# Gate products from GpSimd to VectorE and to an earlier place, the attention's division on ScalarE, and weight sums of the branch projection made in DRAM

## The chip, the cores and the metric

One core of a Trainium2 chip runs the kernel. The metric is the device time of one execution in microseconds (us). The core has five engines with a queue of instructions each: TensorE (PE in the profile, its weight loads PEld), VectorE (DVE), ScalarE (ACT), GpSimd (POOL) and SyncE (SP). Each works its own queue in order and waits for the others by semaphores. SP, ACT and POOL can also issue DMA transfers; a transfer that adds into its destination is issued by POOL here.

## The reference, cut to what matters

```python
shift, scale, gate = jnp.split(silu_c @ w_ada[l] + b_ada[l], 3, axis=-1)
h = _modulate(_rmsnorm(xs, norm_g[l]), shift[:, None], scale[:, None])
p = h @ w_l                       # q, k, v, z_a, u_b, z_b, g_a, g_b: 9216 columns
attn = _attention(q, concat(k, kc), concat(v, vc))     # 12 heads, 4 key heads
y_a = (attn * silu(z_a)) @ w_pa
y_b = (_fourier_mix(u_b) * silu(z_b)) @ w_pb
y = (sigmoid(g_a) * y_a + sigmoid(g_b) * y_b) @ w_o
out = _rmsnorm(xs + gate[:, None] * y, final_g)
```

There are 512 latent tokens, 256 context tokens and 2048 channels; all is float32. `gate` is a vector of 2048 numbers, a product of a row of 2048 with a 2048x2048 matrix. It is used only at the very end, on the output of the last product. This vector is called the modulation gate below, to keep it apart from the branch gates `g_a`, `g_b`.

## The kernel before, in words

**Stages, in order of time.** (1) The start computes shift, scale, the token norms, `h`, and the Fourier branch. (2) Eight groups, g0 to g7 (the table `KINDS`): three of q and z_a, two of g_a, one of keys and values (g5, number `KV`, which also makes the context's), two of g_b. (3) The attention, 48 steps (12 heads, 4 blocks of 128 queries), a loop of 51 turns. (4) Two branch products of `attn * silu(z_a)` with `w_pa` (groups 10 and 11). (5) Two output products with `w_out` (groups 8 and 9) and the final norm.

**A group** multiplies 512x2048 activations by a 2048x1024 slab of weights with seven products instead of eight (a Strassen scheme with the names P1, Q5, P2, Q6, P7, Q3, Q4). Each product has four pieces of weights, 128x1024 numbers or 512 KB each; in the branch products it is three pieces. A float32 matmul is made of three passes over rounded parts: ScalarE makes the high part of a piece (`split_from`, L166, tile `whi`), VectorE the low part (L167, `wlo`), and `mm3` (L318 to L320) issues the three. A piece thus gives 12 matmuls of 512 columns.

**Weights are streamed.** `todo` lists the pieces in order of use. `start_load` (L203) takes the next one, asks SP for its load into a free slot of `raw_pools` (tile `wr`) and puts it on `ahead`; it does so whenever a slot is free. There are four such slots in the pool `wp`, and two more, `raw0` and `raw1`, from the end of the start on; `raw1` is lent out for other things from g4 on, and two slots of the pool `gvp` are added in g6 and g7. Some products use sums of weight blocks: the buffers `R` (`chain`) hold a block to which POOL's DMA adds the next (L273). The fifth product, P7, of the branch groups takes a sum of two blocks: SP loads one into a slot, then POOL issues a DMA that adds the other into the same slot (L206, the argument `onto`).

**The attention loop.** Step i has `scores(i)`: PE multiplies 128 queries with 768 keys, VectorE finds the row's maximum (L1233), ScalarE takes the exponential and the row's sum (L1235). `turn(i-1)` transposes the probabilities on PE (L1251) and splits them (L166, L167, `pth`, `ptl`). `values` multiplies with the values every second step. `divide(i-1)` takes the reciprocal of the sum (L1244) and multiplies it into the 128x128 block of silu(z_a), both on VectorE (L1245). Beside it run the fillers: the 64 parts of `y_b`, for which POOL's queue loads the gates (L1178) and stores the results (L1202), and the loads of the next head's q and z (L1085).

**The modulation gate before.** It is also made in the attention loop, by `gate_unit`. The transposed gate weights come as 32 pieces of 128x1024 (`w_gate`), two for each of 16 blocks. For each block POOL multiplies both pieces with the row silu(c) (L1329, twice), adds them (L1332), and ScalarE sums the result along the row (L1333, `accum_out`). Four such units are issued in three steps from step 2 on, so that the last is issued at step 37. Each piece is asked for with `ask_gate`, out of the order of `todo`, when the piece before it of the same half is taken up.

**Order.** The program is written out by Python loops; the framework's scheduler places the instructions of each engine in an order of its own from the dependencies and its estimates. Branch results are brought back by `branch_done` (a DMA that adds `y_b` from DRAM, L1350) and five ticks later by `turn_merged` (PE transposes, L1359); `job` counts one tick for each piece of weights.

## Time and profile before

| what | us |
|---|---|
| time, median of 3 runs | 1392.07 |
| lowest and highest of the 3 | 1389.04, 1392.32 |
| time of the profiled execution | 1390.56 |
| its span, first to last instruction | 1388.8 |
| PE busy in it | 1302.5 (94%) |
| DVE busy | 1014.4 (73%) |
| ACT busy | 689.6 (50%) |
| POOL busy | 292.2 (21%) |

The busy time of an engine is the time in which it executes, not that in which it waits; matmuls overlap, so that PE shows as busy whenever one is in flight. `PEclk` is the share of full speed that the clock of TensorE was granted. Issuing a DMA isn't counted as busy on SP and ACT. All times of the trace are counted from the start of the span.

### The profile page before, as it was taken

What the parts mean: (1) busy time and instruction counts of PE and PEld (TensorE: products, weight loads), DVE (VectorE), ACT (ScalarE), POOL (GpSimd) and SP (SyncE); (2) the same over time, 40 slices, a digit from 0 to 9 for tenths busy, and PEclk for the clock granted to TensorE, in tenths of its full rate; (3) what the DMA queues carried; (4) which work ended last, traced back from release to release, by engine and by line L of the source; (5) the groups of instructions that cost most, each with busy time, mean ns of one, the idle gap of its engine ahead of it and who ended that gap; (6) DMA issues with size and microseconds to landing.
All of it is one profiled execution on the core that took longest, in us unless ns stands there. A gap on an engine that the chain in (4) does not pass through costs nothing.

```text
span 1388.8 us, 17575 instructions
## 1 busy us (share of the span) xinstructions
PE 1302.5 (94%) x6522; PEld 1062.5 (77%) x6522; DVE 1014.4 (73%) x1277; ACT 689.6 (50%) x1063; POOL 292.2 (21%) x280
## 2 busy tenths in 40 slices
PE   7999999999999999999999986788699997999997
PEld 3676888888888888888888865677688776778885
DVE  4666899878787867474867658687788665778676
ACT  5222565555555545443545544455456544555544
POOL 0110010212110010010201157654630212121310
PEclk9999999999999999999999999899999998999999
DMA  9897687897888899776698775453563898899986
GB/s 386 334 377 287 210 190 249 206 254 201 252 241 247 294 255 284 178 184 200 168 313 229 224 258 165 143 177 108 180 156 100 229 250 178 248 211 222 215 215 176
DMA packets 101990, 312.25 MB, mean 225 GB/s; under 512 B 9616, under 2 KB 32912, under 8 KB 97552
## 3 DMA queue, kind: packets, MB, share of 16 engines
q0 software_dynamic: 28560, 117.46, 36.0%
q1 hardware_dynamic: 48720, 163.65, 34.0%
q10 hardware_dynamic: 24624, 30.02, 6.2%
q8 instruction: 51, 0.84, 0.2%
q14 instruction: 35, 0.29, 0.1%
HBM read 280.15 MB, written 30.94 MB: 224 GB/s over the span
## 4 chain that ended last, share of the span: by engine, by line
PE 75%; DMA 8%; POOL 6%; DVE 5%; issue 3%; ACT 2%; POOLq 0%; SPq 0%; DVEq 0%; ACTq 0%
PE x L319 8%; PE x L320 8%; PE x L318 8%; PE y L319 7%; PE y L320 7%; PE y L318 7%; PE banks L318 6%; PE banks L320 6%; PE banks L319 6%; POOL wr L1329 3%; DMA wr<-in_w_gate 3%; DMA s<-yb_d 3%; POOL wr L1332 2%; PE pd L510 2%; DMA wr<-in_w_pab 2%
## 5 line engine op out<-in xcount | busy, mean ns | idle before, releaser
L167 DVE TENSOR_TENSOR wlo<-R,whi 128x1024 fp32r<-128x1024 f32 x138 | 167.9, 1221 | 90.2 <-ACT whi L166 89.6
L166 ACT ACTIVATE whi<-R 128x1024 fp32r<-128x1024 f32 x138 | 145.9, 1059 | 170.4 <-PE banks L320 46.8
L167 DVE TENSOR_TENSOR wlo<-wr,whi 128x1024 fp32r<-128x1024 f32 (+1 forms) x123 | 150.7, 1229 | 60.9 <-ACT whi L166 60.9
L166 ACT ACTIVATE whi<-wr 128x1024 fp32r<-128x1024 f32 (+1 forms) x123 | 128.4, 1049 | 101.3 <-PE y L320 36.7
L318 PE MATMUL banks<-whi,s 128*128 128x512 f32 x396 | 158.9, 401 | 9.9 <-DVE ev L833 4.9
L319 PE MATMUL banks<-wlo,s 128*128 128x512 f32 x396 | 156.9, 396 | 0.9 <-DVE wlo L167 0.9
L320 PE MATMUL banks<-whi,s 128*128 128x512 f32 x396 | 156.9, 396 | 0.0
L273 POOL DMA_DIRECT2D R<-in_w_g x64 | 55.3, 863 | 419.9 <-DVE wlo L167 234.6
L318 PE MATMUL x<-whi,s 128*128 128x512 f32 x352 | 137.2, 390 | 0.0
L320 PE MATMUL x<-whi,s 128*128 128x512 f32 x352 | 137.0, 389 | 0.0
L319 PE MATMUL x<-wlo,s 128*128 128x512 f32 x352 | 136.9, 389 | 0.0
L318 PE MATMUL y<-whi,s 128*128 128x512 f32 x316 | 123.0, 389 | 0.0
L319 PE MATMUL y<-wlo,s 128*128 128x512 f32 x316 | 122.9, 389 | 0.0
L320 PE MATMUL y<-whi,s 128*128 128x512 f32 x316 | 122.8, 389 | 0.0
L318 PEld LDWEIGHTS banks<-whi,s 128*128 128x128 f32 x396 | 75.6, 191 | 26.3 <-issue 5.3
L166 ACT ACTIVATE s<-wr 128x512 fp32r<-128x512 f32 (+2 forms) x93 | 61.7, 678 | 67.4 <-PE y L319 16.3
L319 PEld LDWEIGHTS banks<-wlo,s 128*128 128x128 f32 x396 | 75.6, 191 | 15.6 <-DVE wlo L167 1.3
L320 PEld LDWEIGHTS banks<-whi,s 128*128 128x128 f32 x396 | 75.4, 190 | 15.6
L167 DVE TENSOR_TENSOR s<-wr,s 128x512 fp32r<-128x512 f32 (+2 forms) x93 | 69.2, 771 | 24.7 <-ACT s L166 24.5
L320 PEld LDWEIGHTS x<-whi,s 128*128 128x128 f32 x352 | 66.1, 188 | 13.8
L319 PEld LDWEIGHTS x<-wlo,s 128*128 128x128 f32 x352 | 66.1, 188 | 13.6
L318 PEld LDWEIGHTS x<-whi,s 128*128 128x128 f32 x352 | 66.1, 188 | 13.6
(289 smaller groups left out, 2986.7 us busy)
## 6 DMA issues: line engine op xcount, KB each, us to landing
wr<-in_w_g SPq DMA_DIRECT2D x128, 512.0 KB, 4.9
R<-in_w_g POOLq DMA_DIRECT2D x64, 512.0 KB, 6.6
wa<-in_w_ss POOLq DMA_DIRECT2D x26, 1024.0 KB, 8.2
R<-in_w_g SPq DMA_DIRECT2D x32, 512.0 KB, 4.9
wr<-in_w_gate SPq DMA_DIRECT2D x32, 512.0 KB, 4.2
wr<-in_w_pab SPq DMA_DIRECT2D x26, 512.0 KB, 5.4
wr<-in_w_o SPq DMA_DIRECT2D x24, 512.0 KB, 7.3
R<-in_w_o POOLq DMA_DIRECT2D x24, 512.0 KB, 7.9
```

The lines of the kernel that those rows point to most:

```text
L166: first = nc.scalar.activation(hi, src, ACT.Copy)
L167: return first, nc.vector.tensor_tensor(lo, src, hi.bitcast(F32), op=ALU.subtract)
L273: nc.gpsimd.dma_start(chain[e.pc], e.nxt, accum_op=ALU.add)
L318: nc.tensor.matmul(o, ah, bh, start=start, stop=False, skip_group_check=cont)
L319: nc.tensor.matmul(o, ah, bl, start=False, stop=False, skip_group_check=cont)
L320: nc.tensor.matmul(o, al, bh, start=False, stop=stop, skip_group_check=cont)
L510: last = nc.tensor.matmul(acc[32 * j : 32 * j + 32, :256], c2[:, 8 * h + k, :], w[:, k, :], start=n < 4, stop=n >= KK - 4)
L1329: nc.gpsimd.tensor_tensor(w, w, crow[part], op=ALU.mult)
L1332: nc.gpsimd.tensor_tensor(w, w, gw[1], op=ALU.add)
```

## The change

It has four parts.

1. **The gate's products move to VectorE.** Each of the 32 pieces is now handled by one instruction, `scalar_tensor_tensor`, which multiplies it by 0.5 and by the row, and sums along the row into a column of `gparts` (`use_gate`, in the new file L1091). POOL's two multiplications and its addition, and ScalarE's summation, are gone; one small addition of the two halves of `gparts` is new.
2. **28 of the 32 move into the groups.** A new table `GATE_AT` names the piece of the product after which a gate piece is used: three each in g1 and g2, one each in g3 and g4, six in g5, six in g6, eight in g7. The piece stands in `todo` behind the weights it follows and takes a slot of `raw_pools` like them. The row's halves are loaded and put through silu in g0 and g1, and in g6. The first half lies in `raw0`, which is no slot for weights from P7 of g0 until the sixteenth gate piece is done in g6; the second half lies in `raw1`. The last four gate pieces stay in the attention, at steps 2 to 22.
3. **The division** in the attention loop, a multiplication of a 128x128 block with a column, goes from VectorE to ScalarE. The reciprocal stays.
4. **The sums for P7 of the branch groups are made early.** In steps 3 to 20 of the attention, `weight_sum` makes six sums of two blocks: POOL loads one block into a free buffer (L1379), adds the other by DMA (L1380), and stores the sum to DRAM (`p7_d`, L1381). P7's pieces then are plain loads of SP from there. `turn_merged` comes six ticks after its result, no longer five.

```diff
+GATE_AT = ([(g, n, 1) for g in (1, 2) for n in ("P2", "Q6", "Q3")] + [(3, "Q5", 1), (4, "P2", 1)]
+           + [(5, n, 1) for n in ("P1", "P2", "Q6", "P7", "Q3", "Q4")] + [(6, n, 1) for n in ONE_GROUP if n != "Q5"]
+           + [(7, n, 1) for n in ONE_GROUP] + [(7, "Q6", 3)])
+    p7_d = dsc.tile([2, 3, P, 1024], F32, name="p7_d")
...
-            if e.onto is not None:
-                nc.gpsimd.dma_start(raw, e.onto, accum_op=ALU.add)
...
-                stream(key, [part(1)], 1024, 2, pc=pc, onto=part(2))
+                stream(key, [p7_d[g - BRANCH_A, pc]], 1024, 2, pc=pc)
...
+                q = None if self.last else GATE_AT.get((self.g, name, pc))
+                if q is not None:
+                    use_gate(q, get(("gate", q)))
+                    if q == KK - 1:
+                        raw_pools.append((rp, 1, "raw0", 1))
...
-    def use_gate(q):
-        w = get_aside(("gate", q))
+    def use_gate(q, w):
         with tc.issue_after(last_split[-1][1].ins):
             nc.vector.scalar_tensor_tensor(w, w, 0.5, crow[q // KK], op0=ALU.mult, op1=ALU.mult,
                                            accum_out=gparts[:, q : q + 1])
...
-        nc.vector.tensor_scalar(z, z, r, None, op0=ALU.mult)
+        nc.scalar.mul(z, z, r)
...
-            nc.gpsimd.tensor_tensor(w, w, crow[part], op=ALU.mult)
-            nc.gpsimd.tensor_tensor(w, w, gw[1], op=ALU.add)
-            nc.scalar.activation(w, w, ACT.Copy, scale=0.5, accum_out=gparts[:, kb : kb + 1])
...
-        after(5, lambda: turn_merged(j, half))
+        after(6, lambda: turn_merged(j, half))
...
+    def weight_sum(n):
+        i, pc = divmod(n, 3)
+        t, w = take((1024,)), BranchWeights(i)
+        part = lambda i: w[CHAIN[i][0], CHAIN[i][1], pc]
+        nc.gpsimd.dma_start(t, part(1))
+        summed.append((t, lambda: nc.gpsimd.dma_start(t, part(2), accum_op=ALU.add),
+                       lambda: nc.gpsimd.dma_start(p7_d[i, pc], t)))
...
+        if 3 <= i < 21:
+            n, step = divmod(i - 3, 3)
+            if step == 0:
+                weight_sum(n)
+            else:
+                summed[-1][step]()
+            if step == 2:
+                give(summed.pop()[0])
+        if 2 <= i < 26 and i % 6 in (2, 4):
+            n, last = NGATE + (i - 2) // 6, i % 6 == 4
+            if not last:
+                ask_gate(n)
+            else:
+                use_gate(n, get_aside(("gate", n)))
```

What it moves is seen in the queues. First POOL, early in the attention, before: `wr` are gate pieces, `crow` and `s_6426` the two halves of the row, `qz_d` is q and z of a head, `g_d` the gates of the filler.

```order
L1329 TENSOR_TENSOR wr_7009<-wr_7009,s_6426 128x1024
L1329 TENSOR_TENSOR wr_7011<-wr_7011,crow_6424 128x1024
L1332 TENSOR_TENSOR wr_7011<-wr_7011,wr_7009 128x1024
L1329 TENSOR_TENSOR wr_7139<-wr_7139,s_6426 128x1024
L1085 DMA s_7014<-qz_d 128x1024
L1329 TENSOR_TENSOR wr_7141<-wr_7141,crow_6424 128x1024
L1332 TENSOR_TENSOR wr_7141<-wr_7141,wr_7139 128x1024
L1329 TENSOR_TENSOR wr_7228<-wr_7228,s_6426 128x1024
L1202 DMA yb_d<-R_1303 128x1024
L1329 TENSOR_TENSOR wr_7230<-wr_7230,crow_6424 128x1024
```

POOL at the start of the attention in the new kernel: `p_d` is the DRAM buffer of the sums, L1379 the load, L1380 the load that adds, L1381 the store, L1099 the load of a head.

```order
L1379 DMA s_6641<-in_w_pab 128x1024
L1200 DMA R_1304<-g_d 128x1024
L1200 DMA R_1305<-g_d 128x1024
L1099 DMA s_6588<-qz_d 128x1024
L1380 DMA s_6641<-in_w_pab 128x1024
L1099 DMA s_6727<-qz_d 128x1024
L1379 DMA s_6773<-in_w_pab 128x1024
L1381 DMA p_d<-s_6641 128x1024
L1380 DMA s_6773<-in_w_pab 128x1024
L1379 DMA s_6883<-in_w_pab 128x1024
L1381 DMA p_d<-s_6773 128x1024
L1099 DMA s_6885<-qz_d 128x1024
```

No arithmetic on 128x1024 is left on POOL there; in its place stand transfers that depend on one another, and the load of a head (`s_6885`) behind them.

Next DVE in g7, at the splits of the chained sums of Q6 and the first of P7, before: L167 is the low part of a split (a piece is split whole into `wlo`, or in two halves into `s`).

```order
L167 TENSOR_TENSOR s_233<-R_1302,s_232 128x2x256
L167 TENSOR_TENSOR s_346<-R_1302,s_345 128x2x256
L167 TENSOR_TENSOR s_494<-R_1303,s_493 128x2x256
L167 TENSOR_TENSOR s_610<-R_1303,s_609 128x2x256
L167 TENSOR_TENSOR wlo_6071<-R_1304,whi_6070 128x1024
L167 TENSOR_TENSOR wlo_6092<-R_1305,whi_6091 128x1024
L167 TENSOR_TENSOR wlo_6111<-wr_6032,whi_6110 128x1024
```

The same place in the new kernel: L174 is the split, L262 the difference of a piece of P7 and its chained sum (L258 before), L1091 the gate.

```order
L174 TENSOR_TENSOR s_234<-R_1303,s_233 128x2x256
L262 TENSOR_TENSOR wr_6148<-R_1303,wr_6148 128x1024
L174 TENSOR_TENSOR s_347<-R_1303,s_346 128x2x256
L1091 SCALAR_TENSOR_TENSOR wr_6032,gparts<-wr_6032,crow_5386 128x1024
L174 TENSOR_TENSOR s_495<-R_1304,s_494 128x2x256
L174 TENSOR_TENSOR s_611<-R_1304,s_610 128x2x256
L262 TENSOR_TENSOR wr_6165<-R_1304,wr_6165 128x1024
L174 TENSOR_TENSOR wlo_6168<-R_1305,whi_6167 128x1024
L174 TENSOR_TENSOR wlo_6186<-R_1306,whi_6185 128x1024
L1091 SCALAR_TENSOR_TENSOR wr_6091,gparts<-wr_6091,crow_5386 128x1024
```

The gate instructions stand between the splits, which queue behind them, and the differences for P7, which stood together ahead of these rows, now stand among them.

Last POOL at the end of the attention, where the branch product begins, before: L1342 loads a gate, L273 adds to a chained sum, L206 adds to a piece of P7, L1350 adds `y_b`.

```order
L1342 DMA s_8874<-g_d 128x1024
L1342 DMA s_8694<-g_d 128x1024
L206 DMA wr_8716<-in_w_pab 128x1024
L273 DMA R_1302<-in_w_pab 128x1024
L1342 DMA s_8929<-g_d 128x1024
L273 DMA R_1303<-in_w_pab 128x1024
L1350 DMA s_8691<-yb_d 128x1024
```

And the same place in the new kernel (L1351, L277 and L1359 are the same lines).

```order
L1351 DMA s_8865<-g_d 128x1024
L1351 DMA s_8687<-g_d 128x1024
L277 DMA R_1303<-in_w_pab 128x1024
L1351 DMA s_8920<-g_d 128x1024
L277 DMA R_1304<-in_w_pab 128x1024
L1359 DMA s_8684<-yb_d 128x1024
```

The L206 row is gone and all else kept its order, so that L1350 no longer stands behind a transfer that waits for SP's load.

More of the change, by code (lines that the diff above doesn't have):

```diff
@@ L412, in block_kernel @@
                     todo.insert(len(todo) - 4 + pc, todo.pop())
+            for pc in range(4):
+                if (g, name, pc) in GATE_AT:
+                    q = GATE_AT[g, name, pc]
+                    stream(("gate", q), w_gate[q], 1024, 1, "raw")
+                    e = todo.pop()
+                    at = next(i for i, x in enumerate(todo) if x.key == (name, g, pc))
+                    todo.insert(at + 1, e)
     for i in range(2):
@@ L1058, in load_row, with silu_of_row @@
     def load_row(half):
-        row = crow[half] = take((1024,)) if half else rp.tile([P, 1024], F32, tag="raw1", bufs=1, name=uid("crow"))
+        row = crow[half] = rp.tile([P, 1024], F32, tag=f"raw{half}", bufs=1, name=uid("crow"))
         nc.gpsimd.dma_start(row, c_row[:, 1024 * half : 1024 * half + 1024].broadcast_to([P, 1024]))
-    def silu_of_row(half):
-        e, row = take((1024,)), crow[half]
+    def silu_of_row(half, e):
+        row = crow[half]
         nc.scalar.activation(e, row, ACT.Tanh, scale=0.5)
         nc.vector.scalar_tensor_tensor(row, e, 1.0, row, op0=ALU.add, op1=ALU.mult)
-        give(e)
     def ask_gate(q):
@@ L1123, in block_kernel @@
         for name in ONE_GROUP:
+            if (g, name) in ((0, "Q4"), (KV + 1, "P1")):
+                assert not any(p[2] == "raw0" for e in ahead for p, _ in e.raws) or g
+                load_row(int(g > 0))
+            elif (g, name) == (1, "Q5"):
+                silu_of_row(0, flat(new_ev()))
+            elif (g, name) == (KV + 1, "P2"):
+                silu_of_row(1, gvp.tile([P, 1024], F32, tag="raw", bufs=2, name=uid("e")))
+            if (g, name) == (0, "P7"):
+                raw_pools.remove((rp, 1, "raw0", 1))
             if (g, name) == (0, "Q5"):
@@ L1167, in block_kernel @@
     fill_acc, b1 = banks[1][:, 0, :], lambda: banks[1][:, 1, :]
-    assert not any(p[0] is gvp or p[2] == "raw1" for e in ahead for p, _ in e.raws)
+    assert not any(p[0] is gvp for e in ahead for p, _ in e.raws)
     todo_gb, gb = [(j, h) for j in CHUNKS for h in range(2)], {}
@@ L1363, in turn_merged @@
         nc.scalar.copy(r.rearrange("p (b k) c -> p b (k c)", b=2), tp)
-    gw = [None, None]
-    for half in range(2):
-        load_row(half)
-    for q in (0, KK):
-        ask_gate(q)
+    def weight_sum(n):
[5 more added lines that the diff above has]
+                       lambda: nc.gpsimd.dma_start(p7_d[i, pc], t)))
+    summed = []
     fill(2)
@@ L1377, in block_kernel @@
                 load_head(h + 2)
-            if i == 1:
-                for half in range(2):
-                    silu_of_row(half)
             if i % 12 == 10 and i // 12 + 1 < NKV:
```

31 lines of the change are left out of this document (10 added, 21 removed).

## The prediction

> **What bounds the kernel now.** I read the profile's page first, for where PE is not busy. The row of 40 slices has 34.7 us to a slice.
>
> ```profile
> span 1388.8 us, 17575 instructions
> ...
> PE   7999999999999999999999986788699997999997
> ...
> POOL 0110010212110010010201157654630212121310
> PEclk9999999999999999999999999899999998999999
> ```
>
> PE is full except at the start, in slices 24 to 29 (the attention) and near slice 34, and POOL is busy just where PE is not. The windows view gives it by stage: busy time of each engine, instructions in brackets, then granted clock, DMA share, GB/s.
>
> ```profile
> core 0: us, PE busy (x) PEld busy (x) DVE busy (x) ACT busy (x) POOL busy (x), PEclk, DMA share, GB/s
> 271.00:346.00 75.00, 75.00 (x333) 62.10 (x332) 60.51 (x69) 39.25 (x73) 12.73 (x12) 1.00 0.81 219
> ...
> 658.00:733.00 75.00, 75.00 (x333) 62.10 (x332) 55.17 (x62) 38.76 (x67) 11.69 (x12) 1.00 0.80 243
> 733.00:808.00 75.00, 75.00 (x333) 62.10 (x332) 51.49 (x54) 38.74 (x47) 11.12 (x16) 1.00 0.84 242
> 808.00:1020.00 212.00, 163.29 (x953) 139.36 (x952) 155.72 (x197) 103.37 (x182) 127.93 (x66) 0.92 0.49 165
> 1030.00:1075.00 45.00, 44.88 (x305) 39.69 (x305) 37.66 (x71) 27.69 (x49) 5.75 (x8) 1.00 0.42 116
> ...
> 1095.00:1250.00 155.00, 138.70 (x624) 113.13 (x623) 101.64 (x90) 75.07 (x75) 32.50 (x41) 0.97 0.91 226
> 1250.00:1388.00 138.00, 129.78 (x569) 106.46 (x568) 101.47 (x104) 69.70 (x100) 22.52 (x27) 0.98 0.84 208
> ```
>
> The groups (271 to 808) are bound by PE: no idle time at all. The attention from 808 to 1020 has PE idle for 48.7 of 212 us and a clock of 0.92; the same loop from 1030 to 1075, past the last gate unit, has PE idle for 0.1 of 45 us at full clock. What PE waits for in the first part is told by the chain that ended last, from 830 us to 900 us (start, duration, piece).
>
> ```profile
> 837.36 3.47 DMA wr<-in_w_gate
> ...
> 875.37 3.80 DMA wr<-in_w_gate
> ...
> 879.31 2.31 POOL wr L1329
> ...
> 882.24 2.40 POOL wr L1329
> ...
> 884.71 2.40 POOL wr L1332
> ...
> 887.12 3.55 DMA wr<-in_w_gate
> ```
>
> It is a ring: a load, two products and an addition on POOL, and the freed slot lets the next load start, 11.75 us after the last. 16 blocks of some 12 us are the 200 us of this stage. The waits say how the ring holds the others: the first row is SP's queue, the second ScalarE, both from 808 to 1020 (total, times, longest).
>
> ```profile
> SPq L203 <- POOL wr L1332: 117.2, 16, 12.9
> ...
> ACT wr L1333 <- POOL wr L1332: 43.9, 13, 5.3
> ```
>
> ScalarE's sum stands in its queue ahead of exponentials and splits, so it stops them for 43.9 us, and VectorE and PE behind them.
>
> **The attention, the main term.** The groups of instructions on VectorE count the steps, first from 808 to 1020, then from 1030 to 1075 (count, busy us, mean ns, idle before).
>
> ```profile
> L1245 DVE TENSOR_SCALAR s<-s,gain 128x128 f32<-128x128 f32 x33 | 37.9, 1150 | 0.9
> L1233 DVE TENSOR_REDUCE gain<-banks 128x1 f32<-128x768 f32 x34 | 32.0, 950 | 11.8 <-PE banks L320 11.8
> ...
> L1233 DVE TENSOR_REDUCE gain<-banks 128x1 f32<-128x768 f32 x12 | 11.3, 952 | 2.4 <-PE banks L320 2.4
> ...
> L1245 DVE TENSOR_SCALAR s<-s,gain 128x128 f32<-128x128 f32 x12 | 3.3, 282 | 0.1
> ```
>
> There is one reduction (L1233) to a step. The view of its line has the first and last start:
>
> ```profile
> L1233 DVE TENSOR_REDUCE gain<-banks x48: 940/950/959, 830.2 to 1074.7; 128x1 f32<-128x768 f32 x48
> ```
>
> The first starts at 830, so 34 steps take about 190 us, 5.6 us each; later 12 steps take 45 us, 3.75 each. At the later pace 34 steps gain 34 x 1.85 = 63 us. PE itself is the bound there, so no more is to be had; and the early steps also carry what the late ones don't (weight and value splits, the four remaining gates, the first steps' latency). **I take 56 us**, a pace of 3.95. The bounds are 0 and 66: the idle 48.7 us, and 0.08 x 212 = 17 us that the clock withholds.
>
> Does another engine become the bound? The division leaves VectorE: 12 x 0.28 = 3.4 of its 37.7 us in the late window, 33 x 1.15 = 37.9 of 155.7 in the early one, where the row takes four times as long beside POOL's products. It gives ScalarE 48 instructions. For their price the nearest row is a 128x128 activation in the groups; for the gate instruction it is the same operation without the sum, on silu(c).
>
> ```profile
> L918 ACT ACTIVATE y<-ev 128x128 f32<-128x128 f32 x32 | 8.8, 275 | 4.4 <-DVE ev L833 3.0 <-ACT y L918 0.7 <-DVE y L922 0.2
> ...
> L1066 DVE SCALAR_TENSOR_TENSOR s<-s,s 128x1024 f32<-128x1024 f32 x1 | 1.2, 1216 | 0.0
> ```
>
> ScalarE: 12 x 0.275 = 3.3 on 27.7 of 45 us, 69%. VectorE: 34.3 of 45, 76%, and four gates, 4.9 us, in the early part. Both stay under PE. The cover is gone only where ScalarE waits in its queue for the reciprocal, with an exponential behind it; that is rival B.
>
> By the Trainium skill, "TensorE: Matmul & The Clock Gate", Part 1, the array falls to half clock after an idle window of some 3.4 us and is back at full clock after one busy window. The trace's 0.92 beside idle time agrees in kind. By the page the 17 us come back by themselves once the gaps are short; if the clock were withheld for another cause, the term could not pass 48.7.
>
> **The 28 gates in the groups.** 28 x 1.22 = 34 us go to VectorE; if the sum along the row cost a pass of its own, like the reduction above (0.95 us for 768, 1.27 for 1024), 70 us. The fullest group that gets three, g1 (271 to 346), goes from 60.5 to 64.2 of 75 us (68.0 with the second price); g7, which gets eight and loses the two silu instructions, from 51.5 to 59 (69). It fits beside PE. The transfers are 0.52 MB each: g7 carries 242 GB/s x 75 us = 18.2 MB at a share of 0.84, full at 288 GB/s, 21.6 MB; the eight bring it to 22.4 MB, 78 us, 3 over. Some of it can be loaded ahead, since the waits show loads waiting for slots, and splits seldom for loads (250 to 800 us; SP's queue, then VectorE).
>
> ```profile
> SPq L203 <- DVE wlo L167: 194.3, 48, 14.7
> ...
> DVE wr L258 <- DMA wr<-in_w_g: 10.2, 7, 4.5
> ```
>
> **I take 2 us lost**; bounds 0 (all hidden) and 76 (rival D). By the Trainium skill, "SBUF — State Buffer", "Summary: rules for kernel authors", loads from HBM run at some 358 GB/s; by that figure I estimate 63 us for g7, and this term would be 0. The share of 0.84 at 242 GB/s doesn't show such room, and the row decides.
>
> **The branch products, 1095 to 1250.** PE is idle for 16.3 us there and the clock is 0.97. The waits in that window:
>
> ```profile
> POOL wr L206 <- DMA wr<-in_w_pab: 24.3, 3, 13.4
> ...
> PE banks L1359 <- DMA s<-yb_d: 14.1, 5, 8.0
> ```
>
> PE waits five times, 14.1 us, for a merged result on its way. Two edits meet it: POOL's queue no longer stops for the P7 loads (24.3 us), behind which the merging transfers stand, and the transposes come a tick later, 12 matmuls x 75/333 = 2.7 us. The tick alone covers at most 2.7 of each wait. **I take 10 us**; bounds 0 and 16.3 + 0.03 x 155 = 21. From 1250 on nothing is touched: 0.
>
> **What the sums cost** is 18 transfers on POOL's queue in steps 3 to 20, instead of 128 us of arithmetic. Their landings have these neighbours from 780 to 1110 (last column: us from issue to landing).
>
> ```profile
> s<-qz_d POOLq DMA_DIRECT2D x10, 512.0 KB, 4.5
> ...
> R<-in_w_pab POOLq DMA_DIRECT2D x7, 512.0 KB, 9.3
> ...
> wr<-in_w_pab POOLq DMA_DIRECT2D x3, 512.0 KB, 6.9
> ```
>
> The DMA share is 0.49 there and loses 28 gate loads, so the bytes cost nothing. The order can cost: rival C.
>
> **Sum.** 1390.56 us for the profiled execution (its span of 1388.8 and 1.8 around it; 1.5 below the median, inside the three runs) - 56 - 10 + 2 = 1326.6: **1327 us**.
>
> **Rivals.** A is the forecast; with its own terms between (63 + 14) and (44 + 5) it gives 1314 to 1342. **B**: the loop stays unevenly paced, since reciprocal, division, exponential and splits wait on each other across two engines. At 4.7 us a step it gains 34 x 0.9 = 31 instead of 56: 1352. For it speaks that the early steps do more; against it the late window, which keeps PE full with the same chain. **C**: POOL's queue falls behind. A sum needs a load (4.5) and an addition (6.9) to land, and some 2 us of issue by my estimate: 13.4 us against three steps of 11.9. Six sums end 9 us late, or 6 x 4 = 24 if additions land in 9.3 us; the load of a head, asked three steps ahead, has 11.9 - 4.5 = 7.4 us to spare. So 2 to 17 us are lost: about 1338. **D, slower**: the gate piece takes a slot and DMA time from the weights behind it, until the split is late by a piece. If each of the 28 costs PE a piece, 2.7 us, that is 76 us, and the time 1390.56 - 66 + 76 = 1401. It decides from 2.4 us a gate on. The full PE rows, the waits for slots and the DMA share below 0.9 speak against it; that g5 runs with two slots fewer speaks for it. **E**: nothing changes, since something else paces the early steps: 1390. The chain and the late window speak against it.
>
> **How the numbers follow.** A 0.68, B 0.14, C 0.12, D 0.04, E 0.02. About 0.3% (4 us) is what a measurement of this kernel can tell from no change. A, B and C are faster: 0.94; E 0.02; D 0.04. The range goes from 1306 (pace 3.75, most of the waits for merged results gone with the clock's share) to 1353, past B's centre; D, E and the slower half of B lie outside.
>
> **What would show it.** No L1329 or L1332 rows, POOL nearly idle in the attention; 48 reductions in about 190 us; PE over 95% busy there at a clock of 0.98 or more; PE at 75 of 75 in each group with VectorE at 59 to 64; PE's transposes of merged results waiting under 5 us in all. It would be wrong if PE waits for splits in g5 to g7, if the steps from 3 to 20 take longer than the later ones behind a head's load, or if the divisions on ScalarE show waits for the reciprocal.

## The result

| | median us | lowest to highest | runs |
|---|---|---|---|
| before | 1390.55 | 1387.48 to 1392.32 | 4 |
| changed | 1352.01 | 1349.20 to 1358.17 | 4 |

The ratio is 0.9731, 95% interval 0.9691 to 0.9771: the change makes the kernel faster, by 38.5 us. The forecast was 1327, 25 us lower; the time lies inside the range of 1306 to 1353, at its upper end. The profiled execution of the changed kernel took 1350.64 us, its span is 1348.6.

The page of the changed kernel, the same rows of 40 slices as before (33.7 us to a slice now):

```profile
span 1348.6 us, 17538 instructions
...
PE   7999999999998999999989999889999999999997
...
POOL 0110011111101011011021111111100202121210
PEclk9999999999998999999999999889999999999998
```

POOL's busy stretch in the attention is gone, and PE is full in most of it. But PE has small dents where it had none. The windows view of the changed kernel (columns as in the prediction) says where:

```profile
346.00:421.00 75.00, 75.00 (x332) 62.14 (x331) 62.76 (x78) 40.41 (x81) 13.43 (x14) 1.00 0.85 240
421.00:496.00 75.00, 70.12 (x301) 57.55 (x301) 58.50 (x92) 38.80 (x58) 6.19 (x8) 0.95 0.86 265
...
658.00:733.00 75.00, 69.45 (x294) 56.29 (x293) 52.11 (x61) 32.77 (x60) 11.35 (x13) 0.95 0.77 222
733.00:808.00 75.00, 73.70 (x326) 60.70 (x324) 50.06 (x61) 32.59 (x41) 7.20 (x9) 1.00 0.91 283
808.00:1020.00 212.00, 200.52 (x1218) 173.09 (x1219) 154.13 (x233) 127.34 (x231) 27.50 (x45) 0.96 0.62 199
1095.00:1250.00 155.00, 151.80 (x686) 124.94 (x686) 116.98 (x100) 82.31 (x85) 27.96 (x34) 0.99 0.91 225
```

The count of matmuls tells more than the busy time. 421 to 496 holds 301 where the full row holds 332: 31 x 75/332 = 7.0 us are missing, though PE idles only 4.88, since the clock falls to 0.95. The DMA share doesn't tell where PE starves: before the change the first two of these stretches had 0.87 and 0.88, more than now, with PE full. The attention, 808 to 1020, has 200.5 us of PE instead of 163.3.

**A ledger in three stretches.** The line of the 48 row maxima, one to a step, gives its first and last start. It cuts a run into what comes before the attention's first maximum (the groups and the change-over), the attention's 47 steps, and the rest. The view of that line in the changed kernel:

```profile
L1255 DVE TENSOR_REDUCE gain<-banks x48: 947/957/960, 854.4 to 1046.3; 128x1 f32<-128x768 f32 x48
```

| stretch | before | changed | difference | forecast |
|---|---|---|---|---|
| to the first maximum | 830.2 | 854.4 | +24.2 | +2 |
| first to last maximum | 244.5 | 191.9 | -52.6 | -56 |
| last maximum to the end of the span | 314.1 | 302.3 | -11.8 | -10 |

The three add up to -40.2, the difference of the spans. Two terms came out close to the forecast. The first did not (its stretch holds the change-over from the groups to the attention as well), and the experiments are mainly about it.

**What PE waits for in the groups.** The chain of work that ended last in the changed kernel, from 400 to 430 us (start, duration, piece):

```profile
417.07 1.22 DVE qr L942
418.31 8.93 DMA qz_d<-qr
427.28 0.05 issue
427.33 0.06 DVE qr L1040
...
427.53 1.23 DVE wlo L174
428.80 0.80 PE x L323
```

A store of q reads the memory `qr`, which VectorE's next instruction (L1040, the context's norm) writes again. The store takes 8.93 us to land, and VectorE, which works in order, holds the split of PE's next weights (L174) behind that wait. The wait was in the kernel before too, 4.1 us (the row of `qz_d<-qr` on VectorE; 6.8 now), and hidden; the median landing of the two stores at this place was 5.5 us then and is 9.1 now. The second place, 694 to 711, shows in SP's queue. First the kernel before, then the changed one, 665 to 707 (start, from the first to the last issue, what, how many):

```profile
666.44 38.68 SPq L203 DMA_DIRECT2D wr<-in_w_g  x12
```

```profile
665.44 0.33 SPq L212 DMA_DIRECT2D R<-in_w_g  x1
666.58 19.20 SPq L209 DMA_DIRECT2D wr<-in_w_g  x4
687.88 0.33 SPq L209 DMA_DIRECT2D wr<-in_w_gate  x1
692.49 14.41 SPq L209 DMA_DIRECT2D wr<-in_w_g  x3
```

Twelve weight loads before; seven now, one load of a block for a chained sum and one gate. In both kernels SP's queue waits there for a store of k (`k_d<-qr`), for 11.9 us before and 13.2 now. The store's two transfers took 17.2 us to land in the median before, with PE full, and 14.7 now: the store came no later, but fewer weights were asked for around it. The waits of the changed kernel from 250 to 815 us show both sides of this. SP's queue first, then the splits (total, times, longest):

```profile
SPq L209 <- DVE wlo L174: 146.0, 46, 13.8
...
SPq L209 <- DVE wr L1091: 61.0, 23, 11.8
```

```profile
ACT whi L173 <- DMA wr<-in_w_g: 28.1, 9, 7.9
DVE wr L262 <- DMA wr<-in_w_g: 23.4, 8, 8.5
ACT s L173 <- DMA wr<-in_w_g: 14.7, 5, 4.4
```

SP waits 61 us, 23 times, for a gate's product to free its slot. The splits wait 66 us for weights; the same three rows gave 14.3 us before. SP's waits of all kinds add up to 498 of these 565 us. Before the change they added up to 500, of which the prediction showed the largest row; the next two are:

```profile
SPq L203 <- DVE s L167: 101.6, 33, 16.2
SPq L203 <- DVE R L252: 62.1, 21, 5.6
```

So the sum of SP's waits doesn't tell a stream that feeds PE from one that doesn't. It tells that free buffers, for the most part, decide when a load starts.

### The profile page after: what moved, and what is told of

It is laid out like the page before. It is cut to its first block, busy times and chain, and to the rows that moved or that the text cites. A ratio compares the mean times of both kernels' runs of the same rounds, so it can differ in the third digit from the quotient of the medians.

```text
span 1348.6 us, 17538 instructions
## 1 busy us (share of the span) xinstructions
PE 1296.9 (96%) x6522; PEld 1057.5 (78%) x6522; DVE 995.4 (74%) x1294; ACT 683.5 (51%) x1079; POOL 179.5 (13%) x244
## 4 chain that ended last, share of the span: by engine, by line
PE 57%; DMA 15%; DVE 13%; issue 11%; ACT 4%; POOL 1%; ACTq 0%; DVEq 0%; SPq 0%; POOLq 0%
PE banks L322 8%; PE banks L324 7%; PE banks L323 7%; PE x L323 4%; PE x L324 4%; PE x L322 4%; DVE wlo L174 4%; DMA wr<-in_w_g 4%; PE y L323 4%; PE y L324 3%; PE y L322 3%; PE pd L521 2%; DVE s L174 2%; DMA cf_d<-qr 2%; PE pb L322 2%
## 5 line engine op out<-in xcount | busy, mean ns | idle before, releaser
L174 DVE TENSOR_TENSOR wlo<-R,whi 128x1024 fp32r<-128x1024 f32 x138 | 167.6, 1222 | 63.6 <-ACT whi L173 63.2
L174 DVE TENSOR_TENSOR wlo<-wr,whi 128x1024 fp32r<-128x1024 f32 (+1 forms) x123 | 148.8, 1214 | 57.8 <-ACT whi L173 57.4
L277 POOL DMA_DIRECT2D R<-in_w_g x64 | 55.4, 866 | 451.1 <-DVE wlo L174 207.7
L174 DVE TENSOR_TENSOR s<-wr,s 128x512 fp32r<-128x512 f32 (+2 forms) x93 | 67.1, 752 | 23.3 <-ACT s L173 22.4
```

The source lines that it names most:

```text
L174: return first, nc.vector.tensor_tensor(lo, src, hi.bitcast(F32), op=ALU.subtract)
L277: nc.gpsimd.dma_start(chain[e.pc], e.nxt, accum_op=ALU.add)
```

## The experiments

Each run was timed in three rounds beside the kernel before. The tables give the median, the ratio with its 95% interval, and the ledger of the profiled execution: the differences from before in the three stretches. One execution's ledger and a median can differ by some us.

### What the gates cost in the groups

**No loads** (e2): the product stays, on the row itself; the 28 pieces of gate weights are left out.

```diff
-                    stream(("gate", q), w_gate[q], 1024, 1, "raw")
...
-                    use_gate(q, get(("gate", q)))
+                    nc.vector.scalar_tensor_tensor(row, row, 0.5, row, op0=ALU.mult, op1=ALU.add, accum_out=...)
```

> The changed kernel without the 28 gate loads inside the groups: each product is still made at its place on VectorE, but on the row of silu(c) itself, so that no slot is taken and 14.7 MB are not moved (the gate weights of these 28 are left out of the result). PE loses some 22 us by the end of the groups in the changed kernel. If loads or slots cause it: the 22 us return, about 1330 us, and PE is full from 271 to 808. If VectorE's 28 products (1.22 us each, 34 us) cause it: nothing returns, 1350 to 1354. If only the buffer of silu(c) causes it: 1343 with the stall at 424 still there.

**No products** (e3): `use_gate(q, get(...))` becomes `get(...)`; the 28 sums are left out.

> The changed kernel with the 28 gate loads in their slots, without the 28 products inside the groups (the sums of these 28 are left out of the result); a slot is free once its load has landed, and so somewhat sooner. If VectorE's products cause the 22 us lost in the groups: about 1330. If the bytes cause it (DMA share 0.86 to 0.91): 1348 to 1353. If it is the time that a slot is held until the product has been made: between the two, 1335 to 1345.

**Slots, few bytes** (e4): `stream(("gate", q), w_gate[q][:, :64], 64, 1, "raw")`, and the product on 64 columns.

> The changed kernel with gate pieces of 64 of 1024 columns inside the groups: the slot is taken and held as long until the product at its place, but 1/16 of the bytes move and the product takes some 0.1 us (960 columns of each of the 28 pieces are left out of the result). If the bytes (or the products) cause the 22 us: about 1330. If the slots cause it, by weights asked for late: 1348 to 1353, with PE waiting for splits at 424 and 806 as before.

**Bytes, no slots**, twice. First (e11) the load goes into the row of silu(c), without a product:

```diff
-                    use_gate(q, get(("gate", q)))
+                    nc.sync.dma_start(crow[q // KK], w_gate[q])
```

> The changed kernel with the 28 gate loads of the groups going into the memory of the row of silu(c) and not into raw slots, issued by the same queue at the products' places, and no products (the sums of these 28 are left out of the result): the bytes without the slots. Without loads it was 1328, with slots and 1/16 of the bytes 1339, with both 1352 to 1355. If bytes and slots add up: about 1340. If the bytes alone cost nothing, and matter only by keeping a slot longer: 1328 to 1331. If the bytes alone cost it: 1350.

Then (e14) with a product of 64 columns on the row ahead of that line, which holds each load at its place.

> The bytes without the slots again, now each load at its place: a product of 64 columns on the row of silu(c) stands at each of the 28 places, and the gate's load goes into that row after it (the sums of these 28 are left out of the result). In the run before, 14 of the loads had moved forward into one group and waited for each other on SP's queue. Without loads 1328, with slots and 1/16 of the bytes 1339, with both 1352 to 1355. If slots and bytes add up: 1338 to 1343. If the bytes alone cost nothing: 1328 to 1332. If a load that waits on SP's queue for a product, with weights behind it, is what costs: 1345 or more, with SP's queue waiting for those products.

**Another buffer** (e1) for the tanh of the row's second half: `silu_of_row(1, flat(new_ev()))`.

> The changed kernel with one buffer moved: the second half of silu(c) is made in a buffer of the eviction ring, as the first half is, and not in the memory that q's rows (qr) leave. Buffer theory: in the changed kernel ScalarE's tanh (L1081) waits 10.67 us at 690 us for the store k_d<-qr to land, with splits of weights behind it, and PE loses 8.8 us between 694 and 711; with the other buffer this stall goes and nothing takes its place: about 1343.5 us, 8 below the changed kernel's 1352. Transfer theory: the stall is one of late landings at a DMA share of 0.77 to 0.91, the next split is late anyway, and the time stays at 1349 to 1353.

| run | median | ratio | to first maximum | attention | rest |
|---|---|---|---|---|---|
| changed | 1352.0 | 0.9731 [0.9691, 0.9771] | +24.2 | -52.6 | -11.8 |
| no loads | 1328.0 | 0.9561 [0.9538, 0.9583] | +3.1 | -58.0 | -7.9 |
| no products | 1354.7 | 0.9733 [0.9704, 0.9762] | +28.4 | -51.3 | -10.2 |
| slots, 1/16 of the bytes | 1339.4 | 0.9636 [0.9614, 0.9657] | +7.8 | -52.6 | -9.2 |
| bytes, bunched | 1363.7 | 0.9805 [0.9770, 0.9840] | +38.9 | -57.6 | -10.8 |
| bytes at their places | 1337.4 | 0.9631 [0.9603, 0.9658] | +17.3 | -58.8 | -10.1 |
| other buffer | 1356.3 | 0.9757 [0.9732, 0.9783] | +25.4 | -52.5 | -8.0 |

The products cost nothing: without them the groups are no better; without the loads alone 21 of the 24 us return. Moving the buffer gains nothing either. In the changed kernel ScalarE's tanh stands for the store of k that still reads this memory, 10.7 us. With another buffer ScalarE waits for the weights themselves, in the run e1 from 685 to 715:

```profile
ACT s L173 <- DMA wr<-in_w_g: 11.9, 2, 6.3
```

The chain of that run says why: SP's queue waits for the same store, and only then fetches the weights (start, duration, piece).

```profile
692.01 14.87 DMA k_d<-qr
...
707.88 5.23 DMA wr<-in_w_g
713.13 0.64 ACT s L173
713.81 0.80 PE x L322
```

So the weights come late there, whichever buffer the tanh has. Of the loads' 21 us, slots with few bytes account for 7.8 - 3.1 = 4.7 by the ledger, and bytes without slots for 17.3 - 3.1 = 14.2. The second is not the bytes alone: there SP's queue stands still for the products that hold the loads at their places, and weights stand behind. SP's waits from 250 to 815 us, first the run with slots and few bytes, then that with bytes:

```profile
SPq L209 <- DVE wr L848: 98.9, 22, 14.7
```

```profile
SPq L843 <- DVE crow L841: 47.0, 16, 12.6
SPq L209 <- DVE crow L841: 38.1, 5, 15.1
```

In both SP waits some 90 us for gate products (in e14 20 us more for the gate loads, which share one row); 4.7 us are lost where little is moved and 14.2 where all is. The larger part thus seems to go with the bytes, but the sizes are not firm, since the ledger's first stretch holds the change-over too. The matmuls from 271 to 808 alone give another division (before, changed, no loads, slots with few bytes, bytes at their places):

```profile
271.00:808.00 537.00, 537.00 (x2373) 444.65 (x2372) 386.35 (x459) 269.55 (x426) 67.47 (x78) 1.00 0.82 236
271.00:808.00 537.00, 524.40 (x2287) 431.44 (x2285) 391.70 (x488) 252.81 (x412) 63.30 (x72) 0.99 0.84 247
271.00:808.00 537.00, 533.54 (x2345) 440.41 (x2344) 413.00 (x513) 267.27 (x424) 62.38 (x73) 1.00 0.81 231
271.00:808.00 537.00, 531.29 (x2333) 438.12 (x2333) 380.45 (x506) 259.75 (x420) 64.74 (x73) 1.00 0.81 229
271.00:808.00 537.00, 520.57 (x2272) 428.84 (x2271) 371.17 (x491) 254.63 (x413) 63.72 (x73) 0.99 0.84 246
```

At 0.226 us a matmul the change loses 86 of them, 19.5 us, and the run without loads 28, 6.3 us. With few bytes it is 40, 9.0 us, and with the bytes but no slots 101, 22.9 us, more than with the change itself. The parts don't add up, so no price for a slot or a byte follows; only that the loads as a whole cost some 13 us here and 21 by the first maximum. How much the bytes would cost without any standing in the queue was not tried cleanly: in e11 14 of the 28 loads moved forward into g1 and waited for one another, and PE lost more than with the change.

The mean rate does not tell it. The changed kernel moves 283 GB/s at a share of 0.91 from 733 to 808 and loses PE time there. The last two groups of e14:

```profile
658.00:733.00 75.00, 67.81 (x292) 55.67 (x291) 48.67 (x62) 32.89 (x60) 12.64 (x13) 0.95 0.71 206
733.00:808.00 75.00, 75.00 (x332) 62.12 (x331) 47.81 (x65) 35.84 (x44) 8.05 (x10) 1.00 0.98 298
```

There, at 298 GB/s, PE is full all the same; the stretch ahead of it has lost 40 matmuls at a share of 0.71. Where PE starves, a single piece is late by a few us; a window's share doesn't show that.

### What the attention gains

**Everything but the gates** (e9): the kernel before with the division on ScalarE, the sums in DRAM and the later tick.

> The kernel before with everything of the change but the gates: division on ScalarE, weight sums in DRAM during the attention, merged results a tick later; the 32 gates stay as ring of load, two products and a sum on POOL in the attention. If that ring paces the attention, its 50 us are not gained: the reductions go on at 5.6 us a step, and only the branch products' 10 to 12 us are, less what the sums cost on POOL's queue between the ring's products: 1378 to 1395. If the division was the pace (1.15 us on VectorE beside POOL's products, 38 us in 34 steps): 1345 to 1360.

**Division back on VectorE** (e7): `nc.scalar.mul(z, z, r)` becomes `nc.vector.tensor_scalar(z, z, r, None, op0=ALU.mult)`.

> The changed kernel with the division of the probabilities back on VectorE. If the attention's 50 us come from POOL's ring of gate units alone: VectorE gets 48 x 0.28 = 13.5 us on 151 of 200 and still stays below PE, so 1350 to 1354. If VectorE's share is what paces the steps, or if the division there costs 1.15 us again: 1362 to 1395.

**Sums at the load again** (e8): no `weight_sum` in the attention; the P7 pieces are streamed with `onto=part(2)` as before; the tick stays at 6.

> The changed kernel with the fifth products' weight sums added at the load again, on POOL's queue behind each P7 load, and no sums in the attention; the merged results are still turned a tick later. If POOL's queue, stopped by those loads, is what held the merging transfers: the 12 us of the branch products are lost again, 1360 to 1364, nearly all of it between 1095 and 1250. If the later tick alone gained them: 1350 to 1354. If the 18 transfers of the sums cost the attention something, up to 6 us less than that.

**Sums later** (e12): `if 24 <= i < 42` in place of `if 3 <= i < 21`.

> The changed kernel with the weight sums begun at step 24 of the attention and not at step 3, where the DMA share is 0.34 and not 0.66 to 0.88. With the sums left out of the attention PE was busy 99.8 of 100 us from 858 to 958 and that run stood 8.6 us better at 1075 us, which it lost again in the branch products. If the sums cost those 8.6 us by POOL's queue in the crowded first half: about 1344. If they cost as much at any place, or their products come late for the branch products: 1350 to 1355.

| run | median | ratio | to first maximum | attention | rest |
|---|---|---|---|---|---|
| all but the gates | 1394.1 | 1.0025 [1.0009, 1.0042] | -1.2 | +11.5 | -10.2 |
| division on VectorE | 1348.3 | 0.9691 [0.9654, 0.9729] | +24.9 | -57.8 | -8.6 |
| sums at the load | 1353.9 | 0.9730 [0.9704, 0.9756] | +20.3 | -57.3 | -2.3 |
| sums from step 24 | 1351.9 | 0.9718 [0.9680, 0.9756] | +22.2 | -47.9 | -8.3 |

With the ring of gate units back on POOL, the attention gains nothing; with the sums on the same queue it takes 11.5 us more, 5.4 us a step. So POOL's ring is what paced it. Where the division stands makes no difference that the times can tell: the intervals overlap, though the ledger has 5.2 us less in the attention with it on VectorE. Its price on VectorE, from 808 to 1020 with POOL nearly idle (run e7):

```profile
L1267 DVE TENSOR_SCALAR s<-s,gain 128x128 f32<-128x128 f32 x41 | 11.5, 285 | 1.0
```

285 ns, against 1150 beside POOL's products. What made the division dear left with the ring; it didn't have to move. The two durations agree with the Trainium skill, "SBUF — State Buffer", "Who interferes with whom": by it `tensor_scalar` can take, in a fast mode, ports that VectorE shares with GpSimd, and whichever engine is second waits. On ScalarE it has another price, in the changed kernel in the same window:

```profile
L1267 ACT ACTIVATE s<-s,gain 128x128 f32<-128x128 f32 x40 | 15.3, 402 | 3.8 <-DVE gain L1266 3.7
```

402 ns, not the 275 that I took from the groups; ScalarE had room for it.

Without the sums the attention takes 57.3 - 52.6 = 4.7 us less. That is not simply their price: with the sums in place, no loads (e2), both runs with bytes alone (e11, e14) and the division on VectorE (e7) gain 57.6 to 58.8 as well. The difference lies in one place, the four steps from the ninth row maximum to the thirteenth: 26.2 us in the changed kernel, 20.6 without the sums, 17.8 to 18.8 in e2, e11 and e14, 20.8 in e7. ScalarE stands there for a weight piece of the branch products, and the splits of the probabilities behind it (the changed kernel, 880 to 909):

```profile
DVE ptl L174 <- ACT pth L173: 6.1, 4, 3.6
...
ACT whi L173 <- DMA wr<-in_w_pab: 3.7, 1, 3.7
...
PE banks L1111 <- DVE ptl L174: 3.3, 1, 3.3
```

This piece's load began at 885.3, when a gate's product on VectorE had ended, and took 7.65 us. So by these runs the stall needs the sums and other edits together; how they make it was not tried further. Begun at step 24 the sums take 9.4 us, but the crowded first half runs nearly as it does without them, and 8 of the 9.4 are lost in the last eight steps. Near 1027 us PE waits 4.2 us there, behind ScalarE, which waits 5.3 for a store of `y_b`.

### What the branch products gain

**The old tick with the new sums** (e18): `after(5, ...)` in place of `after(6, ...)`.

> The changed kernel with the merged results turned at the old tick, the sums made early as in the changed kernel. With sums at the load and the new tick, 2 us of the branch products' 12 were gained. If the sums carry the rest and the tick 2: 1352 to 1356, of it 2 to 4 lost between 1075 and 1250. If only both together gain them: 1358 to 1362.

It took 1358.3 us (0.9765 [0.9734, 0.9795]); the rest gained 2.2 us instead of 11.8. With the new tick and the old sums (e8, above) it was 2.3. So neither edit does it alone; both together gain 12, and on the kernel before, with the gates where they were (e9), 10. The waits of PE for merged results from 1040 to 1210, in this run, are nearly those of before:

```profile
PE banks L1368 <- DMA s<-yb_d: 13.1, 5, 7.0
```

In the changed kernel 2.2 us are left in one such wait, and 2.0 in another gap at 1192.

### Where else the gates can go

**16 in the groups, 16 in the attention** (e5), the latter loaded by POOL's queue:

```diff
+GATE_AT = ([(1, n, 1) for n in ("P2", "Q6", "Q3")] + [(4, "P2", 1)]
+           + [(5, n, 1) for n in ("P1", "P2", "Q6", "P7", "Q3", "Q4")] + [(6, n, 1) for n in ONE_GROUP if n != "Q5"])
...
+            if i == 2 + 2 * (n - NGATE):
+                wg[n] = take((1024,))
+                nc.gpsimd.dma_start(wg[n], w_gate[n])
```

> The changed kernel with 16 gates in the groups (g1 three, g4 one, g5 six, g6 six: none in g2, g3 and g7, which run at a DMA share of 0.86 to 0.91) and 16 in the attention, one to two steps, loaded by POOL's queue into free tiles and not into the raw slots; products on VectorE everywhere. If the 22 us lost in the groups come from transfers and slots, most of them return and the attention, at a DMA share of 0.50 and VectorE at 151 of 200 us, takes 12 more gates (16 us of VectorE) for nothing: 1332 to 1338. If the bytes cost the same wherever they move: 1350. If VectorE then bounds the attention: 1345 or more with the reductions above 4.3 us a step.

**All 32 in the attention** (e6), by the same means, one to a step from step 4 on; the rows of silu(c) are still made in the groups and keep their slots.

> The changed kernel with no gate in the groups: all 32 in the attention, one to each of the steps 2 to 33, on VectorE, loaded by POOL's queue into free tiles. The groups run as in the kernel before, so what they lose is 0 to 2 us. Transfer theory: without any of the 28 loads the groups return 22 us, and the attention pays only where VectorE, at 151 + 28 x 1.31 = 188 of 200 us, comes last: 1330 to 1345. Ring theory for the attention: VectorE instead of POOL keeps the steps under 4.4 us. If instead a product on VectorE stands in the way of the softmax chain by its own length, 28 x 1.31 = 37 us come on top: 1365.

**One slot less** (e10): the kernel before, `raw_pools.remove((rp, 1, "raw0", 1))` in g0, given back at the attention.

> The kernel before with one raw slot less from the end of the first group to the attention (the one that a row of silu(c) takes in the changed kernel), nothing else. In the run with all gates in the attention the groups lost 16 us with no gate in them; what they had left of the change was this slot and the two silu's. If the missing slot causes it: 1396 to 1406, with PE waiting near 497, 623 or 700 us for weights asked for late. If the slots are not short (the weight loads come early enough with one less): 1389 to 1392.

**Groups untouched, all 32 in the attention** (e13): the kernel before with the division on ScalarE and the new tick, no gate and no row of silu(c) in the groups, sums at the load. Against the kernel before:

```diff
-                gate_unit(u)
...
+        for q in range(2 * KK):
+            if i == 2 + q:
+                use_gate(q, wg[q])
+                give(wg.pop(q))
+        for q in range(2 * KK):
+            if i == max(2 + q - 3, 0):
+                wg[q] = take((1024,))
+                nc.gpsimd.dma_start(wg[q], w_gate[q])
```

> The groups as in the kernel before, with all their slots; all 32 gates in steps 2 to 33 of the attention, products on VectorE, loaded by POOL's queue into free tiles three steps ahead; both rows made at the attention's start; weight sums at the load as before, merged results a tick later, division on ScalarE. If slots and loads cause what the groups lose, PE is full from 271 to 808 and the shift at the groups' end is 0 to 2 us. The attention gained 50 with four gates and the sums, 57 with four and no sums, 34 with 32 gates and the sums. If the sums' place on POOL's queue made the difference with 32 gates: 57 less some 6, 1335 to 1341. If VectorE's products stand in the softmax chain: 34 to 41 gained, 1347 to 1356.

**Ten in the groups** (e15): g1 three, g4 one, g5 six; otherwise as e13.

> Ten gates in the groups (g1 three, g4 one, g5 six), where the changed kernel and the one with 16 lost 0 to 3 us, none in g6 and g7, which have all their slots again; 22 gates in steps 4 to 33 of the attention, otherwise as the run with all 32 there. If what the groups lose goes with loads and slots in g2, g6 and g7: 2 to 5 us there. If VectorE's products cost the attention, 22 cost less than 32: between the changed kernel's -50 and the run with 32. Together 1335 to 1348; below 1340 it would beat the changed kernel.

**As e13, sums on VectorE** (e16): `stream(key, [part(1), part(2)], 1024, 2, pc=pc)`.

> The run with the groups as before and all 32 gates in the attention, with the fifth products' weight sums made on VectorE from two loaded pieces, so that POOL's queue neither stops for P7 loads nor carries the sums through the attention. It stood 57 us better at 1075 and gained 1 us in the branch products, where PE waited 14 us for merged results. If POOL's queue, stopped for the P7 loads, holds the merging transfers: 8 to 10 of these return, 1323 to 1327. If two raw slots to a piece make the weights late there instead: 1331 to 1338.

| run | median | ratio | to first maximum | attention | rest |
|---|---|---|---|---|---|
| 16 and 16 | 1347.4 | 0.9687 [0.9661, 0.9713] | +18.5 | -50.0 | -6.8 |
| all in the attention, rows in slots | 1360.5 | 0.9774 [0.9742, 0.9806] | +18.3 | -36.2 | -8.0 |
| before, one slot less | 1406.2 | 1.0106 [1.0075, 1.0137] | -0.7 | +12.2 | +5.4 |
| groups untouched, all in the attention | 1333.5 | 0.9595 [0.9571, 0.9618] | -4.9 | -50.3 | -1.6 |
| ten in the groups | 1333.7 | 0.9605 [0.9575, 0.9635] | -2.7 | -49.2 | -5.7 |
| as e13, sums on VectorE | 1332.1 | 0.9591 [0.9566, 0.9615] | -5.3 | -50.8 | -3.5 |

The last three beat the changed kernel by some 19 us. In e13 the groups are full again; its windows view, from 271 to 815 and in the attention:

```profile
271.00:815.00 544.00, 544.00 (x2408) 450.43 (x2407) 391.75 (x464) 274.30 (x432) 69.88 (x84) 1.00 0.83 238
858.00:958.00 100.00, 96.29 (x631) 82.29 (x629) 90.90 (x155) 61.92 (x123) 16.85 (x32) 1.00 0.63 211
```

VectorE does all 32 products in the attention, at 91% of 100 us, and PE stays over 96%. So VectorE had room there, where the DMA engines had it too. That e6, with the same count, gained 14 us less in the attention lies in something else; it differs by loads two steps ahead instead of three, by the sums between them on POOL's queue, and by the slots that the rows held until then, which were not tried apart. In e5 such a load was late at 838 us, where PE waited 12.1 us while VectorE stood for gates asked for two steps ahead (waits from 826 to 862):

```profile
DVE s L1090 <- DMA s<-in_w_gate: 12.4, 2, 7.5
...
PE banks L321 <- DVE R L1221: 12.1, 1, 12.1
```

Two misses stay open. With one slot less PE idled 4.1 us in the groups and lost 30 matmuls, 6.8 us, which the change-over made good by the first maximum; then the attention, with the old ring, took 12 us more, and why is not settled. And e6 lost 18 us ahead of the attention without a single gate in the groups. The two rows with their slots and their silu are left there, but e2 has them too (it gives one of the slots back in g6) and loses 3. The largest gap of e6 in the groups, 6.4 us at 704, stands behind a tanh that waits for the store of k, which took 17.55 us; the gaps at 497 and 623, 5.1 us together, no run explains. In e16, 8 to 10 us of the branch products should have come back if POOL's queue held the merging transfers; 2 did against e13, and PE still waits there for merged results, 12.2 us in 3 waits.

## Why the prediction was right or wrong

**The attention: right, and for its reason.** Forecast 56, measured 52.6 to the last maximum. The pace is 191.9 / 47 = 4.08 us, and I took 3.95 for the first 34 steps; of the 52.6 us, 48.6 were gained from the first maximum to the 34th (183.3 us before, 134.7 now) and 4.0 in the later steps, where I had put nothing; "48 reductions in about 190 us" came out as 192. PE is at 95% rather than over it, the clock at 0.96 rather than 0.98. The run with the ring back (e9) gains nothing here. The reason given for VectorE's relief was half wrong: the division's 1150 ns were POOL's doing, and moving it gained nothing.

**The sums: rival C's size at its low end, but not its working.** I priced a falling-behind of POOL's queue at 2 to 17 us with a chance of 0.12 and left it out of the sum (the middle of that gives 1336, not the 1338 written there). Without the sums the attention gained 57.3, one more than the forecast, so 4.7 us go with them (e8). But they are lost in one stall behind a weight piece, which four runs with the sums don't show, and not by six sums that end late one after another.

**The branch products: right in size, the working too simple.** 10 forecast, 11.8 measured, "under 5 us" of waits came out as 4.2. I had POOL's queue do most of it and the tick at most 2.7 for each wait. Alone each gains 2 us (e8, e18), so the size came out right by luck as far as the working goes. It looks as if PE waited for whichever of queue and tick is later, so that the two can't be priced one by one; that reading was not tested further.

**The 28 gates in the groups: the step that failed.** "I take 2 us lost" became 24 at the first maximum. The products were rightly priced (1220 ns) and rightly hidden. The error lies in the loads, in the sentence "Some of it can be loaded ahead, since the waits show loads waiting for slots, and splits seldom for loads". The row behind it, 194.3 us of SP's queue waiting for slots, 48 times, was read as room. It says the opposite: while SP's queue waits so, no slot is free, and its waits, most of them for buffers, fill 500 of 565 us, so that what is put into the stream goes in place of weights. That splits seldom waited says only that the stream was in time, not by how much. And I asked for the transfers only whether a group's bytes fit its 75 us, which gave g7 alone 3 us; PE starves by single pieces, at places where a store or a load comes some 4 us later than before or where fewer weights are ahead of it, in stretches with shares from 0.77 to 0.91.

This is rival D's mechanism, "takes a slot and DMA time from the weights behind it, until the split is late by a piece", to which I gave 0.04. I priced it all or nothing, 2.7 us for each of 28 gates; the runs show 21 / 28 = 0.75 us a gate on the average for the loads, and 24.2 / 28 = 0.86 in all. Below the 2.4 us at which it turns the sign, it could still take over a third of the gain, and the sum had no place for that. Shown is that the loads cost it and the products don't (e2, e3). How it divides into slots and bytes stays open, and so does why e6 loses 18 us without any gate there: the average is no price that one gate more or less would have. What I had listed as a sign that the forecast is wrong, "if PE waits for splits in g5 to g7", came true, and in g3 too.

**Rival B** gave 1352, which is the time measured, but by a pace of 4.7 us that is not there: the same number for another reason. That 1352 lies in the range is luck in the same way, since its upper end, 1353, was set for B. From 1250 on nothing was touched, and nothing moved.

## What to carry to other kernels

A load queue that waits for buffers nearly all the time has no free buffer to give: here work added to such a stream took the place of the weights behind it, though the engine and the bandwidth seemed to have a fifth to spare. Look for the stage where the DMA engines are idle and the buffers are free, and place the loads there with the work; here the attention took all 32 gates for some 7 us (-50.3 in e13, against -57.3 in e8 with four gates, both without the sums), and the kernel 1333 us. And price a mechanism at a part of its full cost too, not only at all or nothing.

## What the runs showed of the hardware

The same instruction on the same 128x128 block took 1150 ns on VectorE beside POOL's products and 285 ns without them. A wait of PE cost more than its length: 4.88 us idle at 424 us took 31 matmuls, 7.0 us, with the clock at 0.95 in that window. And single landings vary far more than the mean share: a store of 256 KB, 5.4 us in the median of the groups before, took 8.93 us at shares of 0.85 and 0.86, though the same stretches had 0.87 and 0.88 before; the two transfers of the store of k took 17.2 us in the median before and 14.7 after.
